# Down-projection sums formed a tile ahead and without overwriting values in store, with other places and orders at the opening, the norms and the end

## The chip, the core and the metric

One Trainium2 chip, of which one core is used. The metric is the device time of one execution in microseconds. PE is the matmul engine, DVE the vector engine, ACT the scalar engine, POOL is GpSimd, and SP issues most of the DMAs.

## What is computed

One layer of a decoder on 1024 rows of width 1024 in fp32: a gated feed-forward network, a token mixer, a second feed-forward network, and a last norm. The feed-forward width is 2752.

```python
h = h + 0.5 * swiglu(rms_norm(h, ffn1_norm), ffn1_w_gu, ffn1_w_down)
h = h + hybrid_mixer(rms_norm(h, mix_norm), w_in, ..., w_out)
h = h + 0.5 * swiglu(rms_norm(h, ffn2_norm), ffn2_w_gu, ffn2_w_down)
return rms_norm(h, final_norm)
```

The mixer (sparse attention and a gated recurrence) is touched by the change only where its first weights are loaded and where its output ends.

## The kernel before

Each fp32 value is split in a high and a low part, and a product of two values is three matmuls (`mm3`, L145 to L147; in the down stage L638 to L640). `split` makes the parts: the high one on ACT (L139) or POOL (L137), the low one on DVE (L141). A scheduler orders instructions within each engine by when it thinks that they can start; `late()` lets what stands in it go behind other work. A pool hands out tiles under a tag with a fixed number of buffers: an instruction that writes a tile waits until all readers of the tile that had this buffer before are done. SP's DMAs start in order, so one that waits holds all behind it.

**Up stage.** The hidden width is taken in 22 column tiles j. The first two or three are plain products (`up_plain`), the last, half as wide, is `up_last`, and those between go through `up_rest`, which calls `up_strassen`: seven block products w[0] to w[6] of twelve matmuls each in PSUM banks P, Q and T, where four by four blocks would take eight. DVE adds them up: `pc` (L589, L600), `pd` (L592, L597), `pp` (L604). `step()` between the products makes the weight pieces of the next tile: sums on DVE (L437, L438) and POOL, then splits. The product w[6] goes into bank Q, which L597 has to read first. For each tile j `up_out` makes two tiles `hk`, one for either half of the rows: silu(gate) times up. `hid_put` stores them.

**Sums for the down stage.** The down product is a seven-product scheme as well. Two tiles j make one index m (0 to 10). `hid_put` stores A11 and A21 (even j), A12 and A22 (odd j), and once all four are there, S1 to S4 (L484), each written over one of the four `hk` tiles. A21 itself is not stored. `down_sums` loads the four blocks of the down weight for m (tile `wd`, tag `dr`, four buffers, L498), forms T1 to T4 on DVE in place (L503) and stores them (L504). `up_rest` calls its first half, the loads, before `up_strassen` and its second half, all four sums, behind it; the scheduler moves them in among the steps. All stores go to `hs`.

**Down stage.** `down` runs seven stages n of eleven m. For each m it loads two tiles `dr`, the hidden one (L645) and the weight one (L647 or L653), splits them into four tiles `dw`, and does twelve matmuls into four banks. A dictionary `after` holds what is to be called behind a given (n, m): loads of the rows `h` and, in the first network, in stage 6 the normalization of the first four row groups (`first`) and its transposes (`cols`, L199), and in (5, 2) the load and split of a mixer weight (`third`). In stage 6 of the second network the last `tail` indices m are kept back and done one row group t after the other, so that a group's result (L620) is done before the next; `finish` squares it, makes the reciprocal root (DVE, L158 to L168) and multiplies in two halves (L1552).

**Openings.** The first stage begins with loads of x and of weights, `up_plain` in five groups (two banks, then one each), and row sums for the norm. The second network's opening interleaves the last mixer product (`w_out`: 16 products, cq and i, L692 to L694, DVE adds L1469) with the norm of the first four row groups (`xn`, L183 to L187) and their transposes (`cols`), and then `up_plain` in three groups with `x_cols2` for the other four.

## Time and profile before

| | |
|---|---|
| three runs | 2111.97, 2108.41, 2111.63 us |
| median | 2111.63 us |
| profiled execution | 2110.44 us |
| its span | 2108.4 us |
| PE busy | 2045.9 us, 97% |
| DVE, ACT, POOL busy | 68%, 34%, 24% |

The stages by the timeline: first up stage to about 456 us, first down stage to 690, mixer to 1405, second opening to 1500, second up stage to 1885, second down stage to 2098. A line of the timeline is an instruction with its start, its duration, and in brackets how long the engine stood idle before it and what ended that. Waits are grouped by the waiting instruction and what it waited for. In a window, PE's clock is a share of 2.4 GHz.

### The profile page before, as it was taken

The page shows a single profiled execution, that of the slowest core. Times are in us where ns is not written, and L with a number is a line of the kernel's source. Part 1 is how long each engine was busy: PE and PEld are TensorE (multiplying, and loading weights), DVE is VectorE, ACT ScalarE, POOL GpSimd, SP SyncE. Part 2 cuts the span into 40 slices and gives each one's busy share as a digit, 9 for nine tenths or more (in the row PEclk, how much of TensorE's full clock was granted, in tenths as well). Part 3 has the DMA queues.
Part 4 walks back from the last instruction along what each step waited for, and adds up shares of the span by engine and source line. Part 5 has one row for each costly group of instructions (what it writes and reads, how often), then busy time and mean ns, then how long its engine had stood idle before and what let it go on. Part 6 is the DMA issues. An engine that isn't in the chain of part 4 may idle for free.

```text
span 2108.4 us, 30048 instructions
## 1 busy us (share of the span) xinstructions
PE 2045.9 (97%) x10390; PEld 1658.1 (79%) x10390; DVE 1427.9 (68%) x2926; ACT 722.9 (34%) x1525; POOL 506.7 (24%) x566
## 2 busy tenths in 40 slices
PE   8999999999999999999999999999999999989997
PEld 6778778877877889999876676678877878878886
DVE  6977777547676645766488776646876775547668
ACT  6423233213323222211276554434332333313232
POOL 2132233222232101000144433321121222113221
PEclk9999999999999999999999999999999999999999
DMA  7256654147675220101100111242455653247664
GB/s 260 90 185 219 215 180 150 65 170 249 197 225 168 78 86 21 41 23 32 40 14 30 35 45 44 83 145 81 142 180 208 233 175 108 80 146 280 201 192 150
DMA packets 144664, 277.49 MB, mean 132 GB/s; under 512 B 16096, under 2 KB 37632, under 8 KB 144512
## 3 DMA queue, kind: packets, MB, share of 16 engines
q1 hardware_dynamic: 138896, 262.45, 37.4%
q10 hardware_dynamic: 5616, 13.12, 1.7%
q8 instruction: 82, 1.34, 0.3%
q14 instruction: 70, 0.57, 0.1%
HBM read 199.49 MB, written 76.02 MB: 131 GB/s over the span
## 4 chain that ended last, share of the span: by engine, by line
PE 65%; DVE 12%; DMA 10%; issue 8%; POOL 2%; ACT 1%; SPq 1%; DVEq 0%; POOLq 0%; ACTq 0%
PE b L145 9%; PE b L147 9%; PE b L146 9%; PE b L640 6%; PE b L638 6%; PE b L639 6%; PE b L1130 5%; PE b L1140 3%; DMA hs<-wd 3%; PE b L692 2%; PE b L694 2%; PE b L693 2%; PE b L781 2%; DMA wd<-in_ffn_w_down_dram 2%; DMA hs<-hk 2%
## 5 line engine op out<-in xcount | busy, mean ns | idle before, releaser
L145 PE MATMUL b<-xT,wp 128*128 128x512 f32 x1196 | 470.2, 393 | 25.2 <-DVE pd L597 18.5
L146 PE MATMUL b<-xT,wp 128*128 128x512 f32 x1196 | 467.8, 391 | 0.2 <-DVE xT L329 0.2
L147 PE MATMUL b<-xT,wp 128*128 128x512 f32 x1196 | 467.2, 391 | 0.0
L141 DVE TENSOR_TENSOR dw<-dr,dw 128x512 fp32r<-128x512 f32 x308 | 238.8, 812 | 126.0 <-ACT dw L139 117.0
L145 PEld LDWEIGHTS b<-xT,wp 128*128 128x128 f32 x1196 | 225.8, 189 | 79.1 <-DVE pd L597 20.9
L146 PEld LDWEIGHTS b<-xT,wp 128*128 128x128 f32 x1196 | 225.8, 189 | 47.5 <-DVE xT L329 1.3
L147 PEld LDWEIGHTS b<-xT,wp 128*128 128x128 f32 x1196 | 225.6, 189 | 47.5 <-DVE wp L141 0.2
L638 PE MATMUL b<-dw,dw 128*128 128x512 f32 x616 | 244.1, 396 | 9.2 <-POOL dw L137 5.7
L640 PE MATMUL b<-dw,dw 128*128 128x512 f32 x616 | 242.2, 396 | 1.5 <-DVE dw L141 1.2
L639 PE MATMUL b<-dw,dw 128*128 128x512 f32 x616 | 241.9, 393 | 0.0
L139 ACT ACTIVATE dw<-dr 128x512 fp32r<-128x512 f32 x154 | 96.9, 630 | 287.4 <-PE b L638 192.9
L137 POOL TENSOR_SCALAR dw<-dr 128x512 fp32r<-128x512 f32 x154 | 110.9, 721 | 311.7 <-PE b L640 240.0
L139 ACT ACTIVATE wp<-ws 128x512 fp32r<-128x512 f32 x148 | 93.1, 631 | 239.8 <-PE b L146 232.2
L638 PEld LDWEIGHTS b<-dw,dw 128*128 128x128 f32 x616 | 117.1, 190 | 37.6 <-POOL dw L137 9.7
L640 PEld LDWEIGHTS b<-dw,dw 128*128 128x128 f32 x616 | 116.4, 189 | 31.8 <-DVE dw L141 7.9
L1109 POOL TENSOR_SCALAR P<-P,sm,gate 128x640 f32<-128x640 f32 (+7 forms) x128 | 106.0, 837 | 143.2 <-DVE sm L1107 141.0
L1105 ACT ACTIVATE P<-P,sm 128x64 f32<-128x64 f32 (+8 forms) x192 | 114.8, 599 | 64.5 <-DVE sm L1070 59.6
L639 PEld LDWEIGHTS b<-dw,dw 128*128 128x128 f32 x616 | 117.1, 190 | 23.8
L443 POOL TENSOR_TENSOR ws<-wr 128x512 f32<-128x512 f32 x37 | 51.3, 1388 | 345.9 <-DVE wp L141 318.1
L141 DVE TENSOR_TENSOR wp<-wr,wp 128x512 fp32r<-128x512 f32 (+1 forms) x155 | 116.2, 759 | 17.6 <-ACT wp L139 14.5
L139 ACT ACTIVATE wp<-wr 128x512 fp32r<-128x512 f32 x115 | 72.1, 629 | 159.4 <-PE b L146 140.8
L141 DVE TENSOR_TENSOR wp<-ws,wp 128x512 fp32r<-128x512 f32 x148 | 108.5, 734 | 26.3 <-ACT wp L139 26.2
(287 smaller groups left out, 3845.3 us busy)
## 6 DMA issues: line engine op xcount, KB each, us to landing
dr<-hs SPq DMA_DIRECT2D x242, 256.0 KB, 2.8
wr<-in_ffn_w_gu_dram SPq DMA_DIRECT2D x82, 512.0 KB, 4.5
hs<-hk SPq DMA_DIRECT2D x140, 256.0 KB, 2.0
hs<-wd SPq DMA_DIRECT2D x88, 256.0 KB, 2.9
wd<-in_ffn_w_down_dram SPq DMA_DIRECT2D x84, 256.0 KB, 4.1
dr<-in_ffn_w_down_dram SPq DMA_DIRECT2D x62, 256.0 KB, 4.1
wr<-in_w_in_dram SPq DMA_DIRECT2D x20, 512.0 KB, 4.3
wr<-in_w_out_dram SPq DMA_DIRECT2D x20, 256.0 KB, 2.9
```

Source lines behind the costliest of these rows:

```text
L137: nc.gpsimd.tensor_scalar(out=hi, in0=src, scalar1=1.0, scalar2=1.0, op0=OP.mult, op1=OP.mult)
L139: nc.scalar.activation(out=hi, in_=src, func=AF.Copy)
L141: eng.tensor_tensor(out=lo, in0=src, in1=hi.bitcast(F32), op=OP.subtract)
L145: mm(ps, wh, xh, start=first, stop=False, skip_group_check=skip)
L146: mm(ps, wh, xl, start=False, stop=False, skip_group_check=skip)
L147: mm(ps, wl, xh, start=False, stop=last, skip_group_check=skip)
L638: mm(bs[t][:], hl[:, c], dh[:], start=first, stop=False, skip_group_check=True)
L639: mm(bs[t][:], hh[:, c], dh[:], start=False, stop=False, skip_group_check=True)
L640: mm(bs[t][:], hh[:, c], dl[:], start=False, stop=last, skip_group_check=True)
L1105: nc.scalar.activation(out=rng[br], in_=rng[br], func=AF.Exp, scale=-1.0, bias=m, accum_out=st[:, 6 + br:7 + br])
L1109: (nc.vector if br == 0 else nc.gpsimd).tensor_scalar(out=rng[br], in0=rng[br], scalar1=st[:, 6 + br:7 + br], scalar2=self.gate[:, qb, h * ...
L1130: mm(O[pb, c], v, ts[n][:w, c], start=n < 2, stop=n >= len(blocks) - 2, tile_position=(0, half * 64), skip_group_check=True)
```

## The change

1. `hid_put` forms S3 when A11 and A21 are there, and at the fourth tile S2 over A21's tile, S1 over A11's, S4 over the older of A12 and A22.
2. `down_sums` has six buffers; its loads are issued behind the product of tile j for m = j - j0 - 2, and its four sums run in the next `up_strassen`, one behind each of three steps, the rest behind it. `mixer_consts` (`more`) comes one tile sooner.
3. At the first opening `up_plain` is set up ahead of the loop over the loads, and the first half (o = 0) of its first group is written ahead of that loop's last two steps (kt = 6 and 7).
4. `down` takes the tiles `dr` from two pools in turn (six buffers in each), `dw` of the second network from two pools in turn (8 and 12), and its first copies from the pool of `hk`, which now lives through the stage.
5. In the first down stage the mixer weight is allocated at (2, 2) and loaded in four parts at (3, 2) to (3, 8), no longer `late()`; the transposes come at m = 5 to 10 instead of 3 to 10.
6. In the second opening the transposes start one product later, one of them goes behind the loop, and a plain step goes ahead of the second norm's transposes. The pool of `hk` is made behind the loop.
7. `finish` multiplies the first half by the gain as soon as it is there; at the second, ACT scales the first half and DVE does the second. `tail` is 5 instead of 3.

```diff
@@ hid_put
-        if len(t) == 4:
-            for k, a, b, o, op in (("S1", "A21", "A22", "A22", OP.add), ("S3", "A11", "A21", "A21", OP.subtract),
-                                   ("S2", "A22", "A11", "A11", OP.subtract), ("S4", "A12", "A11", "A12", OP.subtract)):
-                nc.vector.tensor_tensor(out=t[o][:], in0=t[a][:], in1=t[b][:], op=op)
-                put(k, t[o])
+        for k, a, b, o, op in {2: (("S3", "A11", "A21", "A21", OP.subtract),),
+                               4: (("S2", "A22", "A21", "A21", OP.subtract), ("S1", "A21", "A11", "A11", OP.add),
+                                   ("S4", "A12", "A21", "A22" if name == "A12" else "A12", OP.subtract))}.get(len(t), ()):
+            nc.vector.tensor_tensor(out=t[o][:], in0=t[a][:], in1=t[b][:], op=op)
+            put(k, t[o])
@@ down_sums
-                t = pool.tile([128, 512], F32, name=self.nm("wd"), tag="dr", bufs=4)[:]
+                t = pool.tile([128, 512], F32, name=self.nm("wd"), tag="dr", bufs=6)[:]
...
             nc.sync.dma_start(out=H[k][m], in_=o)
-        yield
+            yield
@@ up_plain
                 if o == 0:
                     for k in ks:
                         nc.scalar.activation(out=P[k], in_=V[k][:], func=AF.Copy)
+                    if split and ks is groups[0]:
+                        yield
@@ up_rest
+        sums = iter(())
         for j in range(j0, 21):
             if j < 20:
                 raws[j + 2] = self.up_raw(pool, name, j + 2)
-            sums = self.down_sums(H["wd"], name[:4], H, j - j0) if j - j0 < 11 else iter(())
-            next(sums, None)
-            w = self.up_strassen(cpool, j, w, self.up_pieces(pool, raws[j + 1]) if j < 20 else iter(()), R, H)
-            next(sums, None)
-            if j == j0 + 2 and more:
+            w = self.up_strassen(cpool, j, w, self.up_pieces(pool, raws[j + 1]) if j < 20 else iter(()), R, H, sums)
+            for _ in sums:
+                pass
+            if 2 <= j - j0 < 13:
+                sums = self.down_sums(H["wd"], name[:4], H, j - j0 - 2)
+                next(sums)
+            if j == j0 + 1 and more:
                 more()
@@ up_strassen, behind the steps of w[2], w[3] and w[4]
         step()
+        next(sums, None)
@@ down
             for m in range(11):
-                p, nb = (pool, 4) if n == 0 and m < 2 else (pool2, 11 if wide else 9)
+                i = n * 11 + m
+                p, nb = (pool, 6) if i % 6 < 3 else (pool2, 6)
...
-                p, nb = (pool2, 16) if wide and (n or m > 1) else (pool, 8)
+                p, nb = (pool2, 12) if wide and i % 5 > 1 else (pool, 8)
@@ first opening
         for kt in range(KT):
+            if kt == 6:
+                next(plain)
@@ first down stage
     def third():
-        with net.late():
-            Y["w"] = net.wtile(wp, "w_in", "c")
+        Y["part"] = []
+        Y["w"] = net.wtile(wp, "w_in", "c", Y["part"])
 
     after[6, 1] = first
-    for kt in range(KT):
-        after[6, 3 + kt] = lambda: next(Y["cols"])
-    after[5, 2] = third
+    for m in range(5, 11):
+        after[6, m] = lambda m=m: [next(Y["cols"]) for _ in range(1 + (m in (7, 9)))]
+    after[2, 2] = third
+    for i in range(4):
+        after[3, 2 + 2 * i] = lambda i=i: Y["part"][0](2 * i, 2)
@@ second opening
-            if cq >= 2:
+            if cq * 4 + i > 8:
                 next(cols)
...
     cols = net.x_cols2(rows, "b", 2, xf)
+    next(plain)
     for _ in range(4):
         next(cols)
     next(plain)
     for _ in range(4):
         next(cols)
-    next(plain)
@@ finish
+        if c == 0:
+            nc.vector.tensor_tensor(out=hv, in0=hv, in1=net.gb[:, k], op=OP.mult)
+            return
...
+        nc.scalar.activation(out=y[:, :512], in_=h[tt][:, :512], func=AF.Copy, scale=r)
+        nc.vector.scalar_tensor_tensor(out=y[:, k], in0=hv, scalar=r, in1=net.gb[:, k], op0=OP.mult, op1=OP.mult)
```

What this does to the order is shown at three places. The first is DVE in the middle of the first up stage, within one product of an even j. `wd` are the blocks whose sums are formed, `wp` and `ws` weight pieces, `pd` and `pc` the sums that empty the banks. Before:

```order
L503 TENSOR_TENSOR wd_1635<-wd_1637,wd_1635 128x512
L503 TENSOR_TENSOR wd_1637<-wd_1641,wd_1637 128x512
L141 TENSOR_TENSOR wp_1736<-ws_1733,wp_1735 128x512
L503 TENSOR_TENSOR wd_1641<-wd_1641,wd_1635 128x512
L438 TENSOR_TENSOR ws_1849<-ws_1848,wr_1631 128x512
L503 TENSOR_TENSOR wd_1639<-wd_1639,wd_1641 128x512
L597 TENSOR_TENSOR pd_1648<-b_1644,pd_1648 128x512
L141 TENSOR_TENSOR wp_1754<-ws_1680,wp_1753 128x512
```

After (the changed kernel's L597, L600 of before are L604, L608):

```order
L141 TENSOR_TENSOR wp_1861<-ws_1858,wp_1860 128x512
L503 TENSOR_TENSOR wd_1914<-wd_1916,wd_1914 128x512
L438 TENSOR_TENSOR ws_1963<-ws_1962,wr_1760 128x512
L503 TENSOR_TENSOR wd_1916<-wd_1920,wd_1916 128x512
L604 TENSOR_TENSOR pd_1769<-b_1765,pd_1769 128x512
L141 TENSOR_TENSOR wp_1881<-ws_1801,wp_1880 128x512
L503 TENSOR_TENSOR wd_1920<-wd_1920,wd_1914 128x512
L503 TENSOR_TENSOR wd_1918<-wd_1918,wd_1920 128x512
L608 TENSOR_TENSOR pc_1768<-b_1766,pc_1768 128x512
```

All four sums stood ahead of the `pd` sum; now two stand ahead of it, one piece's split and two sums behind it.

The second is SP in the same stage. L504 are stores of sums, L498 loads of the next blocks, L407 loads of up weights. Before:

```order
L504 DMA hs_172<-wd_1804 128x512
L504 DMA hs_194<-wd_1806 128x512
L504 DMA hs_183<-wd_1810 128x512
L407 DMA wr_2129<-in_ffn_w_gu_dram 128x1024
L504 DMA hs_205<-wd_1808 128x512
L498 DMA wd_1964<-in_ffn_w_down_dram 128x512
L498 DMA wd_1966<-in_ffn_w_down_dram 128x512
L498 DMA wd_1968<-in_ffn_w_down_dram 128x512
L498 DMA wd_1970<-in_ffn_w_down_dram 128x512
```

After:

```order
L504 DMA hs_204<-wd_2085 128x512
L504 DMA hs_172<-wd_2243 128x512
L504 DMA hs_194<-wd_2245 128x512
L504 DMA hs_183<-wd_2249 128x512
L498 DMA wd_2412<-in_ffn_w_down_dram 128x512
L498 DMA wd_2414<-in_ffn_w_down_dram 128x512
L498 DMA wd_2416<-in_ffn_w_down_dram 128x512
L498 DMA wd_2572<-in_ffn_w_down_dram 128x512
L407 DMA wr_2419<-in_ffn_w_gu_dram 128x1024
```

Before, the four loads write the four buffers that the four stores ahead of them read, so each waits for its store. After, three loads of one index m and the first of the next go out together, each into a buffer whose sum was stored in the group ahead; the sums that use them run a tile later.

The third is SP at the turn from the second up stage to the down stage: `hk` are hidden tiles on their way to `hs`, `dr` the first tiles of the down stage, `k` rows of h. Before, behind the last full tile's stores:

```order
L478 DMA hs_13099<-hk_16937 128x512
L478 DMA hs_13121<-hk_17079 128x512
L1540 DMA k_17317<-hspill 128x1024
L645 DMA dr_17383<-hs_13048 128x512
L653 DMA dr_17382<-in_ffn_w_down_dram 128x512
L645 DMA dr_17407<-hs_13049 128x512
L653 DMA dr_17406<-in_ffn_w_down_dram 128x512
```

After, two up tiles earlier (`wr` are still up weights):

```order
L663 DMA dr_17362<-in_ffn_w_down_dram 128x512
L655 DMA dr_17388<-hs_13704 128x512
L663 DMA dr_17387<-in_ffn_w_down_dram 128x512
L655 DMA dr_17486<-hs_13708 128x512
L663 DMA dr_17485<-in_ffn_w_down_dram 128x512
L655 DMA dr_17510<-hs_13709 128x512
L407 DMA wr_16533<-in_ffn_w_gu_dram 128x1024
L478 DMA hs_13720<-hk_16499 128x512
```

The first two indices are loaded early in both; the third (`hs_13048`) stood behind the last stores and a load of rows. Now the first three and two later ones go out between the loads of up weights, and the fourth stands ahead of the last stores, which are issued by ACT.

## Rows read from the trace of the kernel before

**Rows 1.** Waits of PE, whole run: us in total, times, longest.

```profile
PE b L145 <- DVE pd L597: 18.5, 12, 3.8
PE b L638 <- POOL dw L137: 5.7, 3, 5.3
PE b L145 <- POOL wp L137: 5.1, 1, 5.1
PE b L199 <- DVE xn L187: 4.6, 3, 2.2
```

**Rows 2.** Windows of the first up stage; columns in the first line.

```profile
core 0: us, PE busy (x) PEld busy (x) DVE busy (x) ACT busy (x) POOL busy (x), PEclk, DMA share, GB/s
138.00:176.00 38.00, 34.19 (x144) 27.80 (x143) 29.89 (x55) 10.65 (x18) 10.75 (x8) 0.96 0.56 183
330.00:368.00 38.00, 38.00 (x169) 31.46 (x169) 27.07 (x41) 11.93 (x21) 12.96 (x10) 1.00 0.34 108
```

**Rows 3.** Timeline of DVE, 260 to 266 us: start, duration, instruction, idle before.

```profile
260.79 0.69 DVE L503 TENSOR_TENSOR wd<-wd,wd 128x512 f32<-128x512 f32 x1 [1.49 <-DMA wd<-in_ffn_w_down_dram]
262.70 0.69 DVE L503 TENSOR_TENSOR wd<-wd,wd 128x512 f32<-128x512 f32 x1 [1.22 <-DMA wd<-in_ffn_w_down_dram]
...
265.12 0.69 DVE L503 TENSOR_TENSOR wd<-wd,wd 128x512 f32<-128x512 f32 x1
265.72 0.69 DVE L597 TENSOR_TENSOR pd<-b,pd 128x512 f32<-128x512 f32 x1
```

**Rows 4.** Timeline of SP, ahead of those sums.

```profile
255.29 4.44 SPq L498 DMA_DIRECT2D wd<-in_ffn_w_down_dram  x4
```

**Rows 5.** Tile `wd`, 95 to 455 us: ns min/median/max; DVE's idle until loads.

```profile
L503 DVE TENSOR_TENSOR wd<-wd,wd x44: 678/686/1673, 97.9 to 304.1; 128x512 f32<-128x512 f32 x44
...
  DMA wd<-in_ffn_w_down_dram: 22.6, 16
```

**Rows 6.** Windows around four other long waits of PE, columns as above.

```profile
620.00:624.00 4.00, 4.00 (x12) 3.14 (x11) 2.49 (x4) 0.63 (x1) 1.70 (x2) 0.57 0.89 250
647.00:655.00 8.00, 6.63 (x16) 4.55 (x17) 5.55 (x9) 2.30 (x3) 3.29 (x3) 0.57 0.78 261
1422.00:1426.00 4.00, 3.48 (x16) 3.22 (x17) 2.83 (x4) 1.43 (x2) 1.33 (x1) 0.58 0.26 97
1890.00:1894.00 4.00, 3.40 (x9) 2.67 (x10) 1.99 (x3) 0.81 (x2) 1.17 (x2) 0.57 1.00 350
```

**Rows 7.** Waits of DVE, first up stage (95 to 455 us).

```profile
DVE hk L484 <- DMA hs<-hk: 18.7, 9, 4.1
```

**Rows 8.** Timeline of PE in the first down stage, instructions behind a wait.

```profile
458.81 0.47 PE L638 MATMUL b<-dw,dw 128*128 128x512 f32 x1 [0.75 <-DVE dw L141]
460.33 0.50 PE L640 MATMUL b<-dw,dw 128*128 128x512 f32 x1 [0.82 <-DVE dw L141]
619.17 0.47 PE L638 MATMUL b<-dw,dw 128*128 128x512 f32 x1 [1.82 <-DVE dw L141]
648.21 0.69 PE L199 MATMUL b<-ident,xn 128*128 128x128 f32 x2 [2.21 <-DVE xn L187]
```

**Rows 9.** Timeline of PE in the second opening.

```profile
1422.49 0.34 PE L199 MATMUL b<-ident,xn 128*128 128x128 f32 x1 [1.94 <-DVE xn L187]
```

**Rows 10.** Timeline of SP, the first load issued after 1862 us.

```profile
1885.54 0.32 SPq L645 DMA_DIRECT2D dr<-hs  x1
```

**Rows 11.** Timeline of PE, the last matmul.

```profile
2097.44 0.39 PE L640 MATMUL b<-dw,dw 128*128 128x512 f32 x1
```

**Rows 12.** Timeline of DVE at the end: first group's add and `y`, last `y`.

```profile
2091.75 0.69 DVE L620 SCALAR_TENSOR_TENSOR k<-b,k 128x512 f32<-128x512 f32 x1 [1.84 <-PE b L640]
...
2095.56 1.42 DVE L1552 SCALAR_TENSOR_TENSOR y<-k,rs,gb 128x512 f32<-128x512 f32 x2
...
2103.97 1.42 DVE L1552 SCALAR_TENSOR_TENSOR y<-k,rs,gb 128x512 f32<-128x512 f32 x2
```

**Rows 13.** Timeline of POOL at the opening, split of the third tile's weights.

```profile
35.53 3.27 POOL L137 TENSOR_SCALAR wx<-wr 128x512 fp32r<-128x512 f32 x4 [15.96 <-DMA wr<-in_ffn_w_gu_dram]
```

**Rows 14.** Waits of SP, first up stage (95 to 455 us).

```profile
SPq L407 <- DVE wp L141: 101.3, 16, 14.8
```

More of the change, by code (lines that the diff above doesn't have):

```diff
@@ L504, in down_sums, with up_plain @@
             nc.sync.dma_start(out=H[k][m], in_=o)
-        yield
-    def up_plain(self, P, groups, js, ws, R, H):
+            yield
+    def up_plain(self, P, groups, js, ws, R, H, split=False):
         nc = self.nc
@@ L593, in up_strassen @@
         step()
+        next(sums, None)
         self.up_mm(P[:], w[3], 1, False, True)
         step()
+        next(sums, None)
         self.up_mm(Q[:], w[4], 5, False, True)
@@ L598, in up_strassen @@
         step()
+        next(sums, None)
         self.up_mm(T[:], w[5], 2, False, True)
@@ L622, in copies @@
         def copies(bs, tag):
-            out = [pool2.tile([128, 512], F32, name=self.nm(tag), tag=tag, bufs=4) for _ in range(4)]
+            p = H["pool"] if tag == "hk" else pool2
+            out = [p.tile([128, 512], F32, name=self.nm(tag), tag=tag, bufs=4) for _ in range(4)]
             for t in range(4):
@@ L667, in down @@
             if n in (0, 2, 3):
[L668 removed]
+                x = copies(bs, "q" if n else "hk")
                 for t in range(4):
@@ L1496, in body @@
     raws[1] = net.up_raw(wu, name, 1)
+    next(cols)
     rows = net.normed(np_, h, sq)
```

35 lines of the change are left out of this document (17 added, 18 removed).

## The prediction

> **What bounds the kernel now.** I read the waits of PE over the whole run first. PE is the only engine that is nearly always busy, so time is to be had only where it stands idle or runs at the lower clock. The reader is to see few names: 18.5 us in 12 waits for the vector sum `pd` (L597), 5.7 us for POOL's split of a down weight, 5.1 us for one split at the opening, and 4.6 us in three waits of transposes for normalized rows `xn` [rows 1]. Next, the windows of PE. From 138 to 176 us it was busy 34.19 of 38 us at a clock of 0.96, from 330 to 368 us all 38.00. DVE worked nearly as much in both, 29.89 and 27.07 us [rows 2]. DVE is therefore not full; it is late at one point. The timeline of DVE shows the point: two sums of down weights (L503) wait 1.49 and 1.22 us for their loads, two more follow among the splits, and L597 comes last, at 265.72 [rows 3]. PE's next product needs the PSUM bank that L597 empties. The loads are late because SP issues them late: it spent 4.44 us over four of them [rows 4], each going into a buffer that a sum had just been stored from, and over the stage DVE waited 22.6 us for them [rows 5]. Last, I read windows around the other long waits of PE. The granted clock is 0.57 or 0.58 in them [rows 6]: part of each ran at 1.2 GHz instead of 2.4, so such a wait costs about as much again behind it.
>
> I sum against the profiled execution, 2110.4 us, 2.0 us over its span of 2108.4 us. The median of the runs is 2111.6, so 1.2 us are added at the end.
>
> **Sums for the down products, both up stages.** The change spreads each tile's four sums over the steps of a later product, and issues the loads a tile ahead into six buffers instead of four. In the new order the first two sums stand ahead of the instruction that was L597, the other two behind it. By the starts in [rows 3] (265.12 and 265.72) one sum holds DVE 0.6 us. Two of the four no longer stand ahead of L597 (1.2 us), and where the loads are in, the waits of 1.49 and 1.22 us go: L597 comes 3.9 us earlier, which is more than the longest of PE's waits for it, 3.8 us [rows 1]. Recoverable are these 18.5 us and the lower clock from 138 to 176 us [rows 2], 38 x 0.04 = 1.5 us: 20.0 us. The loads still wait for stores that come shortly before them (the SP rows of the change), so I leave two waits of about one microsecond: **18 us**. Bounds: 20 us, and 10 us if every second tile stays late.
>
> S1 to S4: DVE's waits for a store of `hk`, 18.7 us in 9 [rows 7], are those of an add that overwrites what is just being stored. After, S1 to S3 write over tiles stored long before; S4 alone overwrites A12, whose store is issued about two DVE instructions earlier. At worst the same 18.7 us stay, on DVE, which has 8 of 38 us free [rows 2]. Nothing for PE, neither way; with that slack gone it is part of the bound of 10.
>
> **FFN1 down.** Start: PE waits 0.75 and 0.82 us [rows 8] for pieces of the third tile, split late. That tile is now loaded during the up stage, but loads and splits of two mixer weights come ahead on SP, POOL and DVE. Walking the new order from the last up product on, I get about 0.3 us of waiting each at the third and fourth tile: **1 us** gained; bounds 1.6 and a loss of 2, if those loads land late, since SP then stands behind a load that waits for DVE's split of a mixer weight. Later: at 619.17 PE waits 1.82 us [rows 8], while DVE and POOL split such weights. These splits now run at the start of the stage, and nothing else takes their place: 1.82 + 4 x 0.43 at the lower clock [rows 6] = **3.5 us**. At 648.21 transposes wait 2.21 us for `xn` [rows 8]. In the new order they come 24 matmuls later, at 38/169 = 0.225 us each [rows 2] 5.4 us, longer than the wait, and the chain that makes `xn` hasn't moved: 2.21 + 8 x 0.43 [rows 6] = **5.6 us**. For both the cover is the down products themselves; without it the old wait stays.
>
> **FFN2 opening.** Transposes wait 1.94 us at 1422.49 [rows 9] and lose 4 x 0.42 = 1.7 us at the lower clock [rows 6]. They now come 19 matmuls of half the width later, some 2.1 us, so the first row is there when PE arrives, but the last of four, made by the same chain, is not: I leave 0.9 us, which gains 2.7 us. The third wait for `xn`, what is left of the 4.6 us (0.4) [rows 1], is covered by 12 matmuls put ahead of it. Together **3 us**; 1.5 if the clock still falls.
>
> **FFN2 down, start.** POOL's split waits for a load that SP could issue only at 1885.54 [rows 10], behind the last stores of the up stage; PE stands 5.3 us [rows 1]. In the new order the first three tiles are loaded two up tiles earlier, and the fourth is issued ahead of those last stores. Next late would be the fourth, due 36 matmuls or 8.1 us into the stage and issued before it begins. 5.3 + 4 x 0.43 [rows 6] = **7.0 us**; a bound of 5.3 if the clock falls all the same.
>
> **End.** PE's last matmul starts at 2097.44 [rows 11], and the last two `y` multiplications end at 2105.39 [rows 12]: 7.6 us behind PE, because the work of four groups queues on DVE. After, five tiles of products instead of three are left for each group (15 matmuls, 3.4 us apart instead of 2.0), the gain is multiplied in early, and one of two multiplications goes to ACT. The first group alone needed from 2091.75 to 2095.56 until its `y` could start [rows 12], 3.8 us with another group's add in between; with 0.7 for one `y` and 0.4 of queueing that makes 4.9 us: **2.7 us**. Bounds 1.5 and 3.2.
>
> **Opening.** The first groups now run both halves before the next group, so that PE has work in the 5.1 us gap [rows 1]. But POOL's split of the third tile waits for its load until 35.53 [rows 13]; the bytes and their order are the same, and what follows on PE needs them. PE's earlier work only lengthens the wait ahead of that point, to some 4 us. So no gain, and a loss of up to 3.5 us if the clock drops behind that wait as it did from 647 to 655 [rows 6]. I take a **loss of 1 us**.
>
> **Sum**: 18 + 1 + 3.5 + 5.6 + 3 + 7.0 + 2.7 - 1 = 39.8. 2110.4 - 39.8 = 2070.6 for the profiled kind, 2072 for the median.
>
> **The port.** The 44 sums took 686 ns in the median, but one took 1673 [rows 5]: a sum can be held some 1.0 us. The Trainium skill, "SBUF — State Buffer", section "Who interferes with whom", says that a VectorE instruction with two SBUF inputs and a GpSimd instruction that reads SBUF exclude each other, the later one waiting for the whole of the other; spread sums meet more of POOL's work that way. The long one agrees with that, the median shows it to be rare; by the page the sum would come out as the first rival's does.
>
> **Rivals.** (1) *Sums still late.* The loads wait for stores, and the sums stand inside PE's steps. If two of a tile's four sums are held 1.0 us each and its loads come 2 us later than I think, half of the stalls stay: 2072 + 8 = 2080, and 2089 with the lower bounds of the other terms. For it: 22.6 us of waits for loads [rows 5]. Against: DVE's free fifth [rows 2]. (2) *Opening and FFN1 start lose.* The opening loses 3.5 us and the blocked SP 2 us: 2072 + 2.5 + 3 = 2077.5. For it: each wait in [rows 6] drew the lower clock. (3) *Slower.* SP works in order, and a load of up weights (L407) waits for a DVE split, 101.3 us in 16 waits, 6.3 us on average [rows 14]. In the new order such a load stands ahead of the group of stores and loads. Should it hold them so that the sums of all 22 tiles stall PE, the change loses from (20.0 + 21.8) / 22 = 1.9 us of stall per tile on (21.8 are the other gains). I see some 2.5 us of slack, so that is 4.4 us of delay. At 6.3 us a tile stalls 3.8 us: 84 us instead of 20, or 2111.6 + 64 - 22 = 2154. Against: that split precedes the sums on DVE as it is. (4) *It does nothing*: the waits sit where the profile names them and the order shows them moved, so only losses that happen to cancel give 2111.
>
> **How the numbers follow.** Forecast 0.56, rival 1 0.25, rival 2 0.12, rival 3 0.04, no change 0.03. All upper bounds together: 20 + 1.6 + 3.5 + 5.6 + 3.1 + 7 + 3.2 = 44.0, so 2067.6 for the median; the runs scatter by 3.6 us, so 2064. Above, 2090 takes in rivals 1 and 2. The 0.2% that a measurement can tell is 4 us. Faster 0.93, same 0.03, slower 0.04.
>
> **What would show it.** In the profile of after: no wait of PE for `pd` over 1 us, and some 2 us in all; DVE's waits for `wd` loads under 10 us per stage; no stretch of half clock but at the opening and the end; no gap of PE where 619, 648 and the start of FFN2 down were; the last `y` ended under 5.5 us behind the last matmul; one wait of PE of 3 to 5 us between 30 and 37 us. I would be wrong if PE's waits for `pd` still sum to 10 us, or if a new wait for `dr` or `dw` opens at the start of a down stage.

## The result, and the profile after

The changed kernel takes 2133.2 us in the median of four runs (2128.7 to 2134.8), the kernel before 2111.8: 1.0098 times as long, 95% interval 1.0076 to 1.0120. It is **slower by 1%**, where 2072 us and a gain of 1.9% were forecast. Its profiled execution spans 2130.6 us, 22.2 more than before.

First the waits of PE over the whole run of the changed kernel (us in total, times, longest), to be held against [rows 1]:

```profile
PE b L145 <- DVE pd L604: 31.7, 18, 3.4
PE b L647 <- POOL dw L137: 4.3, 2, 2.6
PE b L145 <- ACT wp L139: 3.6, 1, 3.6
PE b L199 <- DVE xn L187: 3.5, 3, 2.2
PE b L146 <- DVE xT L329: 2.9, 1, 2.9
PE b L147 <- DVE wx L141: 2.8, 1, 2.8
```

The name at the top is the one that was to vanish: `pd`, 31.7 us in 18 waits instead of 18.5 in 12. POOL's 5.3 us at the start of FFN2 down and the 5.1 us at the opening are gone, other names stand in their place.

Where the 22.2 us came from is read by stages, from one profiled execution of each kernel. All traces hold 10390 instructions of PE, so the n-th in one does nearly the same work as the n-th in another, and the differences of their starts make a balance. The stages begin at PE's first instruction and are cut at ten others, which in the kernel before start at 90, 402, 512, 631, 698, 1408, 1562, 1842, 1940 and 2097 us (the last matmul). So "FFN1 up" and "FFN2 up" are the middle parts of the up stages, and their ends count with the neighbours. Negative is faster than before. The last two columns are two of the experiments below, the second being the best kernel found.

| stage | before, us | changed | T sums behind `pd` | best |
|---|---|---|---|---|
| first opening | 89.1 | +1.2 | +0.5 | -1.6 |
| FFN1 up | 312.0 | **+14.9** | -13.6 | -12.6 |
| FFN1 down, start | 110.1 | +3.1 | +3.6 | -3.2 |
| FFN1 down, around 619 us | 118.3 | -3.8 | -3.8 | -0.7 |
| FFN1 down, around 648 us | 67.5 | -0.5 | -0.5 | -0.4 |
| mixer | 709.8 | +2.0 | -0.1 | +2.2 |
| second opening | 153.6 | +2.6 | +0.8 | -4.5 |
| FFN2 up | 280.5 | **+10.9** | -8.1 | -7.8 |
| FFN2 down, start | 97.7 | -6.2 | -6.6 | -6.2 |
| FFN2 down, rest | 157.7 | -0.3 | -0.3 | -0.3 |
| last matmul to the end | 11.0 | -1.7 | -1.7 | -1.7 |

The two up stages cost 25.8 us, more than the whole loss. They were to gain 18. (The mixer has no edit; its +2.0 stand around one wait for a load at 787 us and vary from -0.7 to +2.9 among the kernels below, those made from the kernel before included.)

What happens in an up stage shows on DVE. Here are two products that follow each other in the changed kernel: of each the T sums (the sums T1 to T4 of the down weights, L503) that stand ahead of the second add into `pd` (L604, the L597 of before), that add, and a piece of what stands between:

```profile
286.55 0.69 DVE L503 TENSOR_TENSOR wd<-wd,wd 128x512 f32<-128x512 f32 x1 [1.19 <-DMA wd<-in_ffn_w_down_dram]
...
289.32 0.69 DVE L503 TENSOR_TENSOR wd<-wd,wd 128x512 f32<-128x512 f32 x1 [1.48 <-issue]
289.94 0.68 DVE L604 TENSOR_TENSOR pd<-b,pd 128x512 f32<-128x512 f32 x1
...
307.11 0.69 DVE L503 TENSOR_TENSOR wd<-wd,wd 128x512 f32<-128x512 f32 x1 [2.80 <-DMA wd<-in_ffn_w_down_dram]
309.29 0.69 DVE L503 TENSOR_TENSOR wd<-wd,wd 128x512 f32<-128x512 f32 x1 [1.49 <-DMA wd<-in_ffn_w_down_dram]
...
310.50 0.69 DVE L503 TENSOR_TENSOR wd<-wd,wd 128x512 f32<-128x512 f32 x1
311.11 0.69 DVE L438 TENSOR_TENSOR ws<-ws,wr 128x512 f32<-128x512 f32 x1
311.71 0.69 DVE L503 TENSOR_TENSOR wd<-wd,wd 128x512 f32<-128x512 f32 x1
312.31 0.69 DVE L604 TENSOR_TENSOR pd<-b,pd 128x512 f32<-128x512 f32 x1
```

In the first product two sums stand ahead of L604, in the second all four, and each time they wait for their loads (the line at 289.32 names no cause, but it starts 0.07 us after a load landed, at 289.25). So it goes through the middle of the stage, 4 and 2 in turns. PE stalls behind both, for 1.10 us at 290.67 and for 3.04 us at 313.05, and behind the second it runs at the lower clock. Its timeline behind the second product, and windows of PE around this stall and another (columns as in [rows 2]; the clock is the third number from the end of the line):

```profile
313.05 0.50 PE L145 MATMUL b<-xT,wp 128*128 128x512 f32 x1 [3.04 <-DVE pd L604]
```

```profile
313.00:318.00 5.00, 4.95 (x15) 3.94 (x16) 3.66 (x5) 1.32 (x3) 3.58 (x3) 0.66 0.24 61
355.00:363.00 8.00, 6.26 (x16) 4.96 (x17) 5.91 (x10) 1.78 (x3) 4.84 (x4) 0.57 0.34 98
```

The kernel before does otherwise in every second product. This is the product after the one in [rows 3], from the timeline of DVE of the kernel before:

```profile
277.62 0.69 DVE L484 TENSOR_TENSOR hk<-hk,hk 128x512 f32<-128x512 f32 x1 [1.88 <-DMA hs<-hk]
278.23 0.68 DVE L141 TENSOR_TENSOR wp<-ws,wp 128x512 fp32r<-128x512 f32 x1
278.83 0.68 DVE L484 TENSOR_TENSOR hk<-hk,hk 128x512 f32<-128x512 f32 x1
279.44 0.68 DVE L437 TENSOR_TENSOR ws<-wr,wr 128x512 f32<-128x512 f32 x1
280.04 0.69 DVE L484 TENSOR_TENSOR hk<-hk,hk 128x512 f32<-128x512 f32 x1
280.64 0.68 DVE L592 TENSOR_TENSOR pd<-b,pp 128x512 f32<-128x512 f32 x1
281.24 0.68 DVE L484 TENSOR_TENSOR hk<-hk,hk 128x512 f32<-128x512 f32 x1
281.84 0.68 DVE L141 TENSOR_TENSOR wp<-wr,wp 128x512 fp32r<-128x512 f32 x1
282.44 0.69 DVE L141 TENSOR_TENSOR wp<-ws,wp 128x512 fp32r<-128x512 f32 x1
283.16 0.69 DVE L438 TENSOR_TENSOR ws<-ws,wr 128x512 f32<-128x512 f32 x1
283.77 0.69 DVE L597 TENSOR_TENSOR pd<-b,pd 128x512 f32<-128x512 f32 x1
```

The four S sums (L484) stand here, the first of them waiting for a store, and no T sum is ahead of `pd`; the scheduler put all four behind it. The sums ahead of `pd` were 4 and 0 in turns. The changed kernel has taken the S sums and their wait out of this place, and T sums have moved into it.

The loads are late as well. SP in the changed kernel, on the way to the sums at 307:

```profile
298.49 0.33 SPq L407 DMA_DIRECT2D wr<-in_ffn_w_gu_dram  x1
299.89 0.33 SPq L478 DMA_DIRECT2D hs<-hk  x1
300.26 2.53 SPq L504 DMA_DIRECT2D hs<-wd  x4
303.74 2.30 SPq L498 DMA_DIRECT2D wd<-in_ffn_w_down_dram  x4
```

The sums stored at 300.26 were formed between 286.55 and 293.5. Their stores stood behind L407, which waits for a split until 294.79, and behind stores of `hk`. The four loads stand behind these stores, and each of them waits until one of the stores has landed, the first until 303.73, though there are six buffers now. The waits of SP over the first up stage:

```profile
SPq L498 <- DMA hs<-wd: 26.6, 38, 3.8
```

So all 38 loads issued there wait for a store of a sum. DVE waits 26.8 us for loads of `wd` in this stage, in 16 waits (22.6 in 16 before, [rows 5]).

### The profile page after: what moved, and what is told of

The parts are those of the page before. It is cut to its first block, busy times and chain, and to the rows that moved or that the text cites. A ratio compares the mean times of both kernels' runs of the same rounds, so it can differ in the third digit from the quotient of the medians.

```text
span 2130.6 us, 29964 instructions
## 1 busy us (share of the span) xinstructions
PE 2055.1 (96%) x10390; PEld 1664.1 (78%) x10390; DVE 1448.7 (68%) x2928; ACT 728.1 (34%) x1533; POOL 512.5 (24%) x568
## 5 line engine op out<-in xcount | busy, mean ns | idle before, releaser
L145 PE MATMUL b<-xT,wp 128*128 128x512 f32 x1196 | 475.5, 398 | 37.5 <-DVE pd L604 31.7
L145 PEld LDWEIGHTS b<-xT,wp 128*128 128x128 f32 x1196 | 227.9, 191 | 95.8 <-DVE pd L604 40.7
L146 PEld LDWEIGHTS b<-xT,wp 128*128 128x128 f32 x1196 | 228.2, 191 | 50.6 <-DVE xT L329 3.8
L147 PEld LDWEIGHTS b<-xT,wp 128*128 128x128 f32 x1196 | 228.0, 191 | 48.6
L141 DVE TENSOR_TENSOR wp<-wr,wp 128x512 fp32r<-128x512 f32 (+1 forms) x155 | 119.5, 782 | 25.4 <-ACT wp L139 21.4
L443 POOL TENSOR_TENSOR ws<-wr 128x512 f32<-128x512 f32 x37 | 52.2, 1410 | 346.1 <-DVE wp L141 322.1
```

Source lines behind the costliest of these rows:

```text
L141: eng.tensor_tensor(out=lo, in0=src, in1=hi.bitcast(F32), op=OP.subtract)
L145: mm(ps, wh, xh, start=first, stop=False, skip_group_check=skip)
L146: mm(ps, wh, xl, start=False, stop=False, skip_group_check=skip)
L147: mm(ps, wl, xh, start=False, stop=last, skip_group_check=skip)
L443: nc.gpsimd.tensor_tensor(out=s3[:], in0=a11, in1=a21, op=OP.subtract)
```

## The experiments

**Theory A** says that a T sum costs when it stands ahead of the second add into `pd` on DVE, and that the new order of S1 to S4 is what moved the sums there. **Theory B** says that it is the lateness of the loads: a round trip from a sum's store to the next load into the same buffer, and SP's queue. Theories C, D and E are rivals of single steps, named in the expectations. "Changed" is the changed kernel; times are medians against the kernel before in the same comparison (2110 to 2111 us).

**1. T part undone, all else changed.**

```diff
-            w = self.up_strassen(cpool, j, w, self.up_pieces(pool, raws[j + 1]) if j < 20 else iter(()), R, H, sums)
-            for _ in sums:
-                pass
-            if 2 <= j - j0 < 13:
-                sums = self.down_sums(H["wd"], name[:4], H, j - j0 - 2)
-                next(sums)
...
+            sums = self.down_sums(H["wd"], name[:4], H, j - j0) if j - j0 < 11 else iter(())
+            next(sums, None)
+            w = self.up_strassen(cpool, j, w, self.up_pieces(pool, raws[j + 1]) if j < 20 else iter(()), R, H)
+            next(sums, None)
...
```

> The changed kernel with the T part of the change undone: the loads and the four sums T1 to T4 of a tile are written where they stood before, at the start and the end of a product's code, two products earlier; six buffers, the order of S1 to S4 and all else as in the changed kernel. Theory A (order on DVE): what costs is how many of a tile's four sums the schedule puts ahead of the second add into pd, and that is set by the order of S1 to S4, not by where the T sums are written. In this kernel the sums still stand 4 and 2 ahead of it in turns, as in the changed kernel, so PE's waits for pd stay near 32 us and the time near 2133 (2125 to 2138). Theory B (round trip): the loads come late behind the stores of the tile before, and writing them a tile ahead or not must show: pd's waits change by 10 us or more, the time by 15 or more.

Measured: 2125.3 us, 1.0077 [1.0058, 1.0097], `pd` 30.0 us in 17 waits. On DVE the sums stand 4 and 2 ahead as in the changed kernel, so where they are written in the code hardly matters, as theory A says. Against the changed kernel 8 us are gained, of which 6 lie in the up stages (+13.3 and +6.1 against before): the waits are nearly the same, but 17 us of these stages run at 1.2 GHz here, in five stretches, and 27 in the changed kernel.

**2. Order of S1 to S4 as before, all else changed.**

```diff
-        for k, a, b, o, op in {2: (("S3", "A11", "A21", "A21", OP.subtract),),
-                               4: (("S2", "A22", "A21", "A21", OP.subtract), ("S1", "A21", "A11", "A11", OP.add),
-                                   ("S4", "A12", "A21", "A22" if name == "A12" else "A12", OP.subtract))}.get(len(t), ()):
+        if len(t) == 4:
+            for k, a, b, o, op in (("S1", "A21", "A22", "A22", OP.add), ("S3", "A11", "A21", "A21", OP.subtract),
+                                   ("S2", "A22", "A11", "A11", OP.subtract), ("S4", "A12", "A11", "A12", OP.subtract)):
...
```

> The changed kernel with the order of S1 to S4 as before (all four formed behind the fourth product, each over the value just stored), T sums and all else as in the changed kernel. Theory A: the sums now stand 4 and 0 ahead of the second add into pd in turns, as in the kernel before; every second tile stalls, pd's waits fall from 31.7 us to about 18, and with the lower clock behind them the time falls by 15 to 30, to 2103 to 2118. Theory B: the T loads and their stores are untouched, pd's waits stay near 32 and the time at 2133, or above it by the 18.7 us that DVE waited for stores of hk before, if those now matter.

Measured: **2087.7 us**, 0.9896 [0.9879, 0.9913]: some 44 us under the changed kernel, by this edit alone. Its waits of DVE in the first up stage:

```profile
DVE hk L484 <- DMA hs<-hk: 20.0, 10, 3.6
DVE wd L503 <- DMA wd<-in_ffn_w_down_dram: 7.9, 8, 1.8
```

The wait for stores of `hk` is back and costs PE nothing. PE waits 5.8 us for L604 in the whole run. The time lies outside both expectations, and the gain is larger than theory A said: the sums stand 4 and 0 ahead as before, but their loads come less late (7.9 us of waits, not 22.6). So the lateness counts as well.

**3. T sums held behind `pd`, all else changed.** The order of issue on DVE is forced, no wait is added.

```diff
         tt(out=c22[:], in0=Q[:], in1=c22[:], op=OP.add)
-        step()
-        next(sums, None)
+        with self.tc.issue_after(nc.cur_bb.bb.instructions[-1]):
+            next(sums, None)
+            next(sums, None)
+        step()
...
```

(The other two sums stand in the same way behind the add into `pc`, and the calls behind the two earlier steps are gone.)

> The changed kernel with the four sums of a tile held behind the second add into pd (two of them, the other two behind the add into pc that follows it), by the order of issue on DVE alone; loads, buffers and all else as in the changed kernel. Theory A: no sum stands ahead of the add that frees PE's bank; PE's waits for pd vanish (under 3 us in all) with the lower clock behind them, 32 + 15 us: 2086, and 2095 if the adds behind them come late in their place. Theory B: the sums wait as long for their loads as before, only one place later, and hold the adds into pc and pp instead: waits of PE for pc or pp of 15 to 30 us, time 2115 to 2133.

Measured: **2083.5 us**, 0.9879 [0.9857, 0.9901]. One product on DVE:

```profile
288.50 0.69 DVE L602 TENSOR_TENSOR pd<-b,pd 128x512 f32<-128x512 f32 x1 [0.81 <-PE b L147]
289.11 0.68 DVE L503 TENSOR_TENSOR wd<-wd,wd 128x512 f32<-128x512 f32 x1
289.70 0.69 DVE L141 TENSOR_TENSOR wp<-ws,wp 128x512 fp32r<-128x512 f32 x1
290.31 0.69 DVE L503 TENSOR_TENSOR wd<-wd,wd 128x512 f32<-128x512 f32 x1
291.22 0.69 DVE L608 TENSOR_TENSOR pc<-b,pc 128x512 f32<-128x512 f32 x1 [0.23 <-PE b L147]
```

Now DVE waits for PE. The wait for `pd` is 1.2 us in the whole run and no sum waits for a load. The up stages gain 13.6 and 8.1 us: theory A. Theory B's waits for `pc` and `pp` did not come.

**4. The new S order alone, put into the kernel before.**

> The kernel before with one part of the change alone: the new order of S1 to S4. Theory A: in the kernel before, DVE waits for stores of hk ahead of these sums, and in every second product this keeps the four T sums behind the second add into pd. With the new order that wait is gone and 3 and 1 of four T sums stand ahead of that add in turns, while their loads still come late. So this part alone makes the kernel slower: pd's waits from 18.5 to 25 to 35 us, the time from 2110 to 2120 to 2135. Theory C (the new S order hurts only together with loads a tile ahead and six buffers): no change, 2106 to 2114.

Measured: **2137.6 us**, 1.0132 [1.0114, 1.0149]. Waits of PE and of DVE in the first up stage:

```profile
PE b L145 <- DVE pd L597: 19.6, 9, 4.9
```

```profile
DVE wd L503 <- DMA wd<-in_ffn_w_down_dram: 30.5, 10, 5.4
DVE hk L484 <- DMA hs<-hk: 0.5, 1, 0.5
```

It takes DVE's 18.7 us of waiting for stores away [rows 7] and makes the kernel 27 us slower, 3 us above theory A's range. The sums stand 3 and 1 ahead, and DVE waits 30.5 us for their loads. Theory C falls.

**5. The T part alone, put into the kernel before, with four buffers as before.**

> The kernel before with the T part alone: loads a tile ahead, the sums spread over the steps of a later product; four buffers and the order of S1 to S4 as before. Theory A: the T sums stay behind the second add into pd in every second product, and in the others 3 stand ahead of it with their loads a tile earlier; pd's waits fall from 18.5 to about 6 us as in the run with the old S order, the time from 2110 to 2092 to 2100. Theory C (the T part gives nothing, what the run with the old S order gained came from the other parts): 2106 to 2114.

Measured: 2119.3 us, 1.0042 [1.0028, 1.0057], outside of both expectations. PE waits 10.7 us for the second add into `pd` and 9.2 us for the first: in every second product three of four sums stand ahead of the second add, one of them (two in FFN2) ahead of the first as well, and DVE waits 18.6 us for loads in the first up stage. With four buffers each load still writes the buffer that a sum has just been stored from.

**6. The T part alone with six buffers.** As 5, and:

```diff
-                t = pool.tile([128, 512], F32, name=self.nm("wd"), tag="dr", bufs=4)[:]
+                t = pool.tile([128, 512], F32, name=self.nm("wd"), tag="dr", bufs=6)[:]
...
-                p, nb = (pool, 4) if n == 0 and m < 2 else (pool2, 11 if wide else 9)
+                p, nb = (pool, 6) if n == 0 and m < 3 else (pool2, 11 if wide else 7)
```

> The run with the T part alone (2119, with four buffers), now with six buffers for the down weights of the up stage (the first pool of FFN1 and FFN2 down takes three tiles instead of two, the second seven buffers instead of nine in FFN1). In every second product all four T sums stand ahead of the second add into pd, in the others none: no better a place than in the kernel before. Theory A with lateness (a sum ahead of pd costs only what its load is late): with six buffers a tile's first loads no longer wait for the stores of the tile just before, so the sums come on time; the up stages gain 8 and 6 us as in the run with the old S order: 2110 - 14 = 2096, range 2092 to 2101. Rival E (the place alone decides): the pattern is the one of the kernel before, 2106 to 2114, or 2119 as with four buffers.

Measured: **2091.9 us**, 0.9916 [0.9900, 0.9931], at the lower end of theory A's range. Two more buffers are worth 27 us (20 in the profiled executions). Sums stand 4 and 0 ahead, as in the kernel before; DVE waits 10.0 us for their loads in the first up stage, not 22.6, and SP's loads wait 11.0 us for stores of sums (10.8 in run 2, 26.6 in the changed kernel). Rival E (the place alone decides) falls: a sum ahead of `pd` costs what its load is late.

**7. Eight buffers in the changed kernel** (`bufs=8` in `down_sums`; the down stage's first pool takes four of six tiles and its second pool has four buffers, since eight beside the six there are more than SBUF holds).

> The changed kernel with eight buffers for the down weights of the up stage instead of six, so that a tile's loads write where the sums of two tiles ago were stored from, never those of the tile just before (the down stage keeps 12 pairs in all: eight buffers in the first pool and four in the second). Theory A: the sums still stand 4 and 2 ahead of the add into pd; the loads still stand behind the same stores on SP; the time stays within 6 us of 2133. Theory B (round trip from store to load): DVE's waits for wd loads fall by more than half, pd's waits from 31.7 to under 15, the time to 2090 to 2110.

Measured: 2113.8 us in ten runs that spread widely (2102.5 to 2119.3), 1.0019 [1.0003, 1.0034]. That is 19 us under the changed kernel and between the two theories: FFN1 up still loses 8.4 us, FFN2 up gains 1.8. But the edit does not do what it was made for: in the first up stage 36 of 38 loads still wait for a store of a sum, 24.8 us in all (26.6 in the changed kernel), and DVE waits 25.6 us for its loads (26.8). So it is no test of theory B. What fell is PE's waits for `pd`, from 31.7 to 23.5 us, and the time of the up stages at 1.2 GHz, from 27 to 10 us. The sums are still in the way, 4 and 2.

**8. T sums held behind `pd` in the kernel before,** nothing else: four buffers, old S order, loads where they were.

> The kernel before with one thing changed: each tile's four T sums are issued on DVE behind the second add into pd of the product that they are written in (two of them) and behind the add into pc that follows (the other two). Loads at the same place, four buffers, the old order of S1 to S4, nothing else of the change. Theory A (the place of the sums decides): PE's waits for pd vanish (under 3 us), the up stages gain 18.5 us and the lower clock behind them as in the run with the T sums behind pd (13.5 and 8.1 us there): 2110 - 21 = 2089, range 2086 to 2094. Theory B (lateness of the loads decides; six buffers and the loads a tile ahead are needed): the sums still wait for loads that wait for stores, now ahead of the adds into pc and pp: waits of PE for those, 2100 to 2115.

Measured: **2088.5 us**, 0.9892 [0.9875, 0.9909], as forecast. FFN1 up -13.0, FFN2 up -8.5, `pd` 1.4 us. DVE waits 25.0 us for stores of `hk` in the first up stage, more than before, and PE doesn't see it.

**9. The same with the new S order.**

> The run before this one with the new order of S1 to S4 as well. Alone, that order cost 27 us. Theory A: it cost them only by letting T sums move ahead of pd; where these are held behind it, the order costs nothing: the same time as the run before this one within 4 us, some 2089. Rival D (the new S sums stand in the way themselves, on DVE or by their stores on SP): 10 us or more above it.

Measured: 2088.0 us, 0.9895 [0.9880, 0.9910]. The S order that cost 27 us alone costs nothing that the time shows once the T sums are held. Rival D falls.

The nine runs and the two kernels in one table. "Ahead" counts the T sums that stand ahead of the second add into `pd`, in two products that follow each other; the up stages are against before.

| kernel | S order | buffers | ahead | FFN1 up, FFN2 up, us | time, us |
|---|---|---|---|---|---|
| before | old | 4 | 4, 0 | 0, 0 | 2110 |
| 4: S alone | new | 4 | 3, 1 | +13.9, +12.7 | 2137.6 |
| 5: T alone | old | 4 | 3, 0 | +6.1, +1.6 | 2119.3 |
| 6: T alone | old | 6 | 4, 0 | -4.8, -7.6 | 2091.9 |
| changed | new | 6 | 4, 2 | +14.9, +10.9 | 2133.2 |
| 1: changed, old T | new | 6 | 4, 2 | +13.3, +6.1 | 2125.3 |
| 7: changed | new | 8 | 4, 2 | +8.4, -1.8 | 2113.8 |
| 2: changed, old S | old | 6 | 4, 0 | -8.2, -6.5 | 2087.7 |
| 8: before, held | old | 4 | 0, 0 | -13.0, -8.5 | 2088.5 |
| 9: before, held, new S | new | 4 | 0, 0 | -11.4, -8.3 | 2088.0 |
| 3: changed, held | new | 6 | 0, 0 | -13.6, -8.1 | 2083.5 |

**10. Three places outside the up stages,** on top of 3: the mixer weight back at its old place, all transposes held behind the products written ahead of them, and at the second opening the plain step back behind the transposes.

> The run with the T sums behind pd (2083), with three places outside the up stages changed as well, each read off from its own stage. (1) The first mixer weight is loaded and split where it was before, in the sixth stage of FFN1 down: the 3.6 us lost at the start of FFN1 down come back and the wait of 1.8 us at the split, 3.8 us with the lower clock, returns: 0 in all. (2) All transposes of xn are held behind the products written ahead of them: in the changed kernel two transposes still stood at their old place and waited 2.21 us; with them behind 24 to 36 more products the wait goes, 4 to 5 us gained. (3) At the FFN2 opening the group of up products goes back behind the transposes: PE's wait of 3.62 us for the first pieces goes, 3.5 us gained, unless the 2.5 us that the opening gained are lost with it. Sum: 2083 - 8 = 2075; 2080 if (3) cancels.

Measured: 2079.5 us, 0.9850 [0.9833, 0.9866]. The sum, 2075, is missed by 4 us. (1) went the way expected, by more: the start of FFN1 down is 6.8 us better than in 3 (3.6 expected), around 619 us it is 5.1 worse (3.8). (2) wrong: the transposes no longer wait, but a product does, for a split that stands behind the same chain on DVE:

```profile
635.17 0.77 PE L650 MATMUL b<-dw,dw 128*128 128x512 f32 x1 [2.91 <-DVE dw L141]
```

(3) right, and more: the second opening gains 4.5 us against before, where 3 lost 0.8.

**11. Mended.** On top of 3: the plain step as in 10, and the mixer weight in four parts that are not issued earlier than written.

```diff
+    def part(k):
+        with net.late():
+            Y["part"][0](k, 2)
...
-        after[3, 2 + 2 * i] = lambda i=i: Y["part"][0](2 * i, 2)
+        after[3, 2 + 2 * i] = lambda i=i: part(2 * i)
```

> The run with the T sums behind pd (2083) with two places outside the up stages mended, each read off from its own stage: the four quarters of the first mixer weight are issued in the fourth stage of FFN1 down, one every second tile, none of them earlier (no load of it stands on SP ahead of the first tiles of the down stage, and no splits come in one block): the 3.6 us lost at the start of FFN1 down come back, and no wait opens at the quarters, 3 to 5 us gained. And the group of up products at the FFN2 opening stands behind the transposes, which gained 5.2 us in the run before. Sum: 2083 - 4 - 5 = 2074, range 2070 to 2080.

Measured: 2077.0 us, 0.9842 [0.9827, 0.9857], inside the range. In the profiled run the start of FFN1 down gains 3.2 us, around 619 us 1.0 is left of 3.8.

**12. Mended, with the old first opening.**

> The run with all mended (2077) with the opening as before: the first groups of up products run both halves one after another only after all splits of the opening are written, as in the kernel before. If the opening's new order costs what the profiles say (0.4 to 1.3 us more than before in most, 5.2 in one), the time falls by 1 to 3 us, to 2074 to 2076. If it had gained in the mean what it meant to, 2078 or more.

Measured: **2073.5 us**, 0.9824 [0.9811, 0.9837], the best kernel of the study, 1.8% faster than before and 0.5 us below what was expected. The interval overlaps that of 11, so the 3.5 us for the opening are likely, not shown. Windows of the two, 30 to 50 us, mended first, old opening second (the profiled execution of 11 is the one whose opening lost 5.2 us; the other kernels with the new opening lost 0.4 to 1.3):

```profile
30.00:50.00 20.00, 16.10 (x48) 10.68 (x47) 14.22 (x32) 9.40 (x16) 2.41 (x4) 0.74 0.48 172
```

```profile
30.00:50.00 20.00, 18.91 (x79) 14.26 (x78) 17.36 (x37) 12.44 (x20) 3.79 (x4) 1.00 0.53 189
```

The new opening breaks PE's one long wait into several. In this execution the clock is low from 17.8 to 24.6 us and again from 38.2 to 48.5. The old opening keeps the wait of 4.4 us at 16.6 us; its clock is low around it, from 14.6 to 21.4 us, and full from there on.

## Why the prediction was wrong, step by step

**S1 to S4: "Nothing for PE, neither way".** This step failed, and it alone turns the sign: the same edit costs 27 us in the kernel before (4) and some 44 in the changed one (2). The cost of the S sums themselves was rightly put at nothing (8, 9). What was missed is that the place which they left, with DVE's 18.7 us of waiting [rows 7], had kept the T sums behind `pd` in every second product. The change was asked for what it removes; what moves up into the gap was not asked. Without this edit (2) the time, 2087.7 us, lies inside the range, yet 16 us over the forecast: by the balance the start of FFN1 down loses 4.6 us there instead of gaining 1, the place around 648 us gains 0.4 instead of 5.6, the second opening loses 0.9 instead of gaining 3, and the two up stages gain 14.7 instead of 18.

**Sums for the down products: +18, measured -25.8.** The order of DVE was compared in one product of before and one of after: four sums ahead, then two. Both kernels have two kinds of products in turns, and the change was from 4 and 0 to 4 and 2. Four less two looked like a gain because unlike products were compared. The size of the prize was right: with the sums out of the way some 22 us come back (21.7 in 3, 21.5 in 8), against the bound of 20. Loads a tile ahead into six buffers bring part of what was said of them as long as the S order is old (6: 12.4 us of the 18).

**The slower rival.** It had the loads held on SP behind L407 and 4% of the chance. SP's waits in L407 did grow, from 101.3 [rows 14] to 141.0 us, and the stores and loads did stand behind them. But with the old S order (2) the loads stand on the same queue, L407 waits 93.0 us, and PE's waits for L604 are down to 5.8 us. So late loads are part of the cause; the rival's price was too high (18 stalls of 1.8 us, not 22 of 3.8), and it named the lateness but not the order on DVE. Whether L407 makes the loads late or waits longer because PE stalls is not shown: no run issues the loads ahead of it or from another engine.

**FFN1 down, start: +1, measured -3.1.** Below the bound of a loss of 2. The bound had SP standing behind loads of mixer weights that wait for splits. That happened: SP issues seven of them (L268) ahead of the fourth tile of the down stage, and stands for splits and for loads. From the waits of SP from 455 to 480 us and the timelines of SP, POOL and PE of the changed kernel:

```profile
SPq L268 <- DVE wl L141: 5.5, 3, 2.4
SPq L268 <- DMA wr<-in_w_in_dram: 5.1, 3, 3.2
```

```profile
457.85 13.88 SPq L268 DMA_DIRECT2D wr<-in_w_in_dram  x7
478.86 0.71 SPq L663 DMA_DIRECT2D dr<-in_ffn_w_down_dram  x1
```

```profile
476.06 0.66 POOL L137 TENSOR_SCALAR dw<-dr 128x512 fp32r<-128x512 f32 x1
```

```profile
476.77 0.50 PE L647 MATMUL b<-dw,dw 128*128 128x512 f32 x1 [2.63 <-POOL dw L137]
486.47 0.50 PE L647 MATMUL b<-dw,dw 128*128 128x512 f32 x1 [1.67 <-POOL dw L137]
```

But the fourth tile came in time, and the longer wait is at the third, which had been loaded during the up stage: its split at 476.06 stands on POOL behind the splits of the mixer weights, which waited there for their loads. The other wait is at the fifth tile, whose weights were requested only at 478.86, after the mixer weights and 4.0 us of waiting for a store of `hk`. The forecast took 0.3 us at the third and fourth tile; what it left out is POOL's waits for the mixer weights. With these weights loaded later the loss goes (10, 11). **619 us: +3.5, measured +3.8**: right.

**648 us: +5.6, measured +0.5.** Wrong twice. Two of the first four transposes stayed at their old place, only the other two moved 24 matmuls on, and the wait is word for word the old one, 2.21 us:

```profile
663.53 0.44 PE L199 MATMUL b<-ident,xn 128*128 128x128 f32 x2 [2.21 <-DVE xn L187]
```

And with all of them held (10) a split for the next product is late by 2.91 us: it stands behind the chain on DVE from the last add to `xn`. So moving the transposes alone gained nothing.

**Second opening: +3, measured -2.6.** The first wait shrank (0.47 and 0.81 us instead of 1.94, where 0.9 was forecast), but the plain step that was put ahead of the second norm's transposes shifts their work on DVE to the end. There PE waits for pieces of the first Strassen product:

```profile
1515.76 0.69 PE L145 MATMUL b<-xT,wp 128*128 128x512 f32 x1 [3.62 <-ACT wp L139]
```

Putting that one step back gained 5.2 us (10 against 3). The prediction had counted these twelve matmuls as cover for a wait of 0.4 us and not asked what comes later by them.

**FFN2 down, start: +7.0, measured +6.2** (bound 5.3), and a wait of 0.39 us is left: right. **End: +2.7, measured +1.7**: within the bounds. The last `y` starts 4.8 us behind the last matmul's start, at 2126.16 and 2121.35, and ends 5.2 us behind its end, where 4.9 was forecast and 7.6 stood before; 0.7 us of that is lost behind it, where the last two stores are under way together. **Opening: -1, measured -1.2**: the size is right by luck, since the form was not: there was no wait of 3 to 5 us between 30 and 37 us, but 2.94 at 18.8 and 2.77 at 40.5.

**The port.** The T sums took 692 ns in the median and 1662 at most in the changed kernel's first up stage, nearly as before [rows 5]. But four of the 44 took over 1.6 us, where one did before, and the same in the second up stage; each of these eight begins while a sum on POOL runs that started 0.55 us earlier (L443, two inputs). The Trainium skill, "SBUF — State Buffer", section "Who interferes with whom", says that a VectorE instruction with two SBUF inputs contends with a GpSimd instruction that reads SBUF. The trace agrees with that, and with the prediction that spread sums meet it oftener. All eight stand behind L604, so they are no part of PE's waits for `pd`.

Of the signs named, three came true (619, the start of FFN2 down but for 0.39 us, the end). "PE's waits for `pd` still sum to 10 us" was one of the two marks of a wrong prediction, "a new wait for `dw` at the start of a down stage" the other. Both are seen.

Open is why the scheduler puts a sum where it does. It orders by its own estimate of when an instruction can start, and no trace shows that estimate; that the S order moves the T sums is seen, why by two places in one kernel and by one in another isn't.

## What to carry to other kernels

Work that nobody waits for (a sum that only feeds a later stage) belongs behind the instruction that frees the bottleneck's buffer, and should be held there by the order of issue. Holding them there gained 22 us in the kernel before, more than the 18 that this part of the change had been made for, with four buffers and the loads where they were (8). Before a wait on a side engine is removed, look at what the scheduler will put into the gap, in every kind of iteration that the loop has, not in one. A load "a tile ahead" is ahead only if it has a buffer that is free by then: in the changed kernel every load still waited for a store issued just ahead of it.

## What the runs showed of the hardware

Waits of DVE that stand behind the bottleneck's needs cost nothing that the time shows, even 25 us of them in one stage (8), and less waiting of DVE for stores of `hk` made the kernel slower (4: 0.5 us instead of 18.7, and 27 us lost, as T sums moved up and their waits for loads grew from 22.6 to 30.5 us). PE's lower clock came with the longer waits: twelve of the changed kernel's fourteen waits of 1.9 us and more have a stretch at 1.2 GHz behind or in them; between the run's beginning and its end there is no other. In the up stages that is 27 us at half speed, so that 31.7 us of waits cost some 14 us more (an estimate: half of the 27). In the first up stage of the changed kernel a load of `wd` took 3.6 us in the median from issue to landing (4.1 before), and a store of a sum 4.5 us (2.8 before), so that a load that waits for a store lands some 8 us after that store was issued (an estimate: the sum of the two). The four loads issued from 303.74 on, for sums whose turn on DVE came at 304.3, landed from 306.99 on.
